# Merged loads and stores for queries, keys and mixed channels, and norm_g spread by TensorE in a one-core hybrid attention layer

## The chip, the cores and the metric

The kernel runs on one core of a Trainium2 chip. The metric is the time in microseconds (us) of one execution on the device. A core has five engines with a queue of instructions each, worked off in order: TensorE (PE in the profile; its weight loads are PEld), VectorE (DVE), ScalarE (ACT), GpSimd (POOL) and SyncE (SP). In this kernel SP issues all the DMA transfers.

## The reference, cut to what matters

One layer over 1024 tokens of 1024 channels, float32:

```python
h = rmsnorm(x, norm_g)
z = h @ w_in                                   # 1024 x 3886 columns, split in 14 parts
a = pool_mixer(pv) * silu(pg)                  # windows of 2, 4, 8, 16, mean minus the token itself
b = dsa_mixer(dq, dk, dv, iq, ik, iw) * silu(dg)   # 6 heads of 64, each query attends to its top 256 keys
c = fox_mixer(fq, fk, fv, log_sigmoid(ff + bf)) * silu(fg)   # 6 heads of 64, causal, forgetting bias
out = rmsnorm(x + concat([a, b, c]) @ w_out, final_g)
```

The top 256 keys of a query are found from an index score, a weighted sum over 8 heads of relu(iq . ik), among the keys of its own chunk of 64 tokens and those before it.

## The kernel before, in words

**Numbers.** Every float32 operand of a product is split into a high part (float32r, made by ScalarE) and a low part, the rest (made by VectorE or GpSimd). A product is then three passes of TensorE (`mm3`, L460): high by high, high by low, low by high.

**Planner.** `Plan` holds all instructions with a duration, a priority and the keys that they read and write. `schedule` is a list scheduler: at each step it takes, over all engines, the instruction that can start first by its prices, with the priority among those of one engine. The order that results is the order in which each engine's queue is filled. A DMA is priced by an issue time on SP (0.45 us in `ld`), a delay, its bytes by a rate (330 GB/s) and a landing time. Tiles have slots (a tag with a size, an offset and a number of slots); a tile that takes over a slot waits for the work on the one before.

**Stages.** First the tokens are normalised in 8 tiles of 128 (`norm`): the square sum on ScalarE (L509 for tile 0, L505 for the others), a multiplication with the factor and with `gb`, norm_g spread over 128 partitions (L515, VectorE, by halves), transposes (L522, TensorE), and the split into `hT` (L526, L527). `gb` is filled in two ways: its first half by a product of a row of ones with the row of norm_g (L415) and a copy (L417, ScalarE), its second half by a DMA that reads the same 2 KB for each of the 128 partitions (L418). Until the first tile is ready, 60 small products on constants (L408) run on TensorE at the lowest priority.

Then come the index scores (`idx_tile`), their top 256 (`search`: 32 rounds of counting, L772 on ScalarE and L777 on VectorE), and beside them the projections with the channels on the partitions (`chan`, 48 products of 512 columns for each 128 channels): keys and queries (`qkproj`), gates (`gate`) and the pool's values. `qkproj` makes the high part `nh` (L723) and the low part `nl` (L724) of 128 channels (a pair of heads) by 512 tokens and stores them to DRAM with two DMAs. `gate` applies tanh on ScalarE (L737) and a VectorE step (L739) in a tile `th`, of which there are two slots, and stores it. The pool mixer (`pool_tile`) loads the gate back into a tile `th`, multiplies (L1093) and stores the result to a DRAM tile `mx_p`.

Attention runs in 12 units: 2 kinds (f, d) x 3 pairs of heads x 2 halves g of the queries (512 tokens each). A unit needs the query tiles `qx` (high) and `ql` (low), both of shape 128 x 2 x 512, where index 1 is the head; each head's 64 channels are loaded into both halves of the partitions, so `load_q` issues 8 DMAs of 128 KB. The key tile `ks` holds for each head its high part in one half of the partitions and its low part in the other (`load_k`, 4 DMAs of 128 KB for 512 keys). The products L925 (with `qx`) and L928 (with `ql`) then give the logits; L936 (VectorE) adds the bias or mask and takes the maximum, L947 is the exponential, L962 the transposes, L969 and L971 the split of the weights, L975 and L980 the products with the values. At its end a unit multiplies with the gate and the softmax denominators, and stores 128 channels by 512 tokens to a DRAM tile `mx_f` or `mx_d`.

The output projection (`outproj`) takes 128 tokens at a time: 8 DMAs of 64 KB bring the 8 blocks of 128 channels from the 8 DRAM tiles, L1133 (ScalarE) and L1134 (GpSimd) split them, 48 products follow, L1146 adds x, and the final normalisation ends in a store.

Of the kernel before, what the change touches and what calls it, by code (L numbers as in the profile page):

```python
# [27 lines left out]
D = 1024  # L28
# [52 lines left out]
class Plan:  # L81
# [81 lines left out]
    def schedule(self):  # L163
# [10 lines left out]
        while len(order) < n:  # L174
# [49 lines left out]
            if e == SP:  # L224
                free[e] = t + o.dur
                st = max(t + 1.4, dma_free[0])
                dma_free[0] = st + o.bytes / 330e3
                o.end = dma_free[0] + 0.7
            else:
                free[e] = t + o.dur  # L230
                o.end = t + o.dur
# [60 lines left out]
def tile_trunk(ctx: ExitStack, tc: tile.TileContext, x, w_in, norm_g, pool_w, pool_scale,  # L292
# [15 lines left out]
    r1 = lay("R", 0, [("hT", 32 * KB, 2), ("Wh", 4 * KB, 2), ("Wl", 4 * KB, 2), ("nh", 2 * KB, 2), ("nl", 2 * KB, 2)])  # L308
# [4 lines left out]
    r3 = lay("R", r2, [("ks", 4 * KB, 3), ("qx", 4 * KB, 2), ("ql", 4 * KB, 2), ("ph", 2 * KB, 3), ("pl", 2 * KB, 2)], 2)  # L313
# [93 lines left out]
    for q in range(60):  # L407
# [3 lines left out]
    grow = P.new("gr", [1, 640])  # L411
    ld(lambda: grow()[:, :512], lambda: norm_g[0:1, 0:512], 2048, w=[(grow, 0)], pr=-101)
    G(lambda: nc.gpsimd.memset(grow()[:, 512:640], 1.0), 60, [], [(grow, 1)], -99)
    pb = P.new("pj", [128, 512])
    P.op(PE, lambda: nc.tensor.matmul(pb(), grow()[:, 512:640], grow()[:, 0:512], start=True, stop=True), 1.7,  # L415
         [(grow, 0), (grow, 1)], [pb], -99)
# [443 lines left out]
    mix_d = {}  # L860

    def load_k(kind, pair, u, pr):
        d = QKD[kind, pair, u]
        k = P.new("ks", [128, 2, 512], F32R)
        kk = [("qk", kind, pair, u, j) for j in range(2)]
        for e in range(2):
            ld(lambda e=e: k()[64 * e:64 * e + 64, 0, :], lambda e=e: d[e, 0:64, :], 131072, kk, [(k, 3 + e)], pr)
        ld(lambda: k()[0:64, 1, :], lambda: d[1, 64:128, :], 131072, kk, [(k, 1)], pr)
        ld(lambda: k()[64:128, 1, :], lambda: d[0, 64:128, :], 131072, kk, [(k, 2)], pr)
        return k  # L870

    def load_q(kind, pair, u, pr):
        d = QKD[kind, pair, u]
        kk = [("qk", kind, pair, u, j) for j in range(2)]
        qx = P.new("qx", [128, 2, 512], F32R)
        for s in range(2):
            for e in range(2):
                ld(lambda s=s, e=e: qx()[64 * e:64 * e + 64, s, :], lambda s=s: d[0, 64 * s:64 * s + 64, :], 131072,
                   kk, [(qx, s, e)], pr)
        ql = P.new("ql", [128, 2, 512], F32R)  # L880
        for s in range(2):
            for e in range(2):
                ld(lambda s=s, e=e: ql()[64 * e:64 * e + 64, s, :], lambda s=s: d[1, 64 * s:64 * s + 64, :], 131072,
                   kk, [(ql, s, e)], pr)
        return qx, ql
# [9 lines left out]
    def unit(kind, pair, g, ks, VV):  # L895
# [3 lines left out]
        qx, ql = load_q(kind + "q", pair, g, pr0)  # L899
        sm = P.new("sm", [128, 4, 2, 2])  # L900
        os = []
        for hd in range(2):
# [11 lines left out]
            for j in range(3, -1, -1):  # L914
                t = 4 * g + j
                Ps.insert(0, [])
                for u in range(g + 1):
# [6 lines left out]
                    kk = [(k, 3), (k, 4)] if hd == 0 else [(k, 1), (k, 2)]  # L924
                    M(lambda s=s, k=k, n=n, j=j, hd=hd: nc.tensor.matmul(  # L925
                        s()[:, :n], qx()[:, hd, j * 128:j * 128 + 128], k()[:, hd, :n], start=True, stop=False),
                      n, kk + [(qx, hd, 0), (qx, hd, 1)], [s], pr)
                    M(lambda s=s, k=k, n=n, j=j, hd=hd: nc.tensor.matmul(  # L928
                        s()[:, :n], ql()[:, hd, j * 128:j * 128 + 128], k()[:, hd, :n],
                        start=False, stop=True), n, kk + [(ql, hd, 0), (ql, hd, 1)], [s], pr)  # L930
# [118 lines left out]
    def pool_tile(m, consts):  # L1049
# [37 lines left out]
        for u in range(2):  # L1087
# [35 lines left out]
    def outproj(i, WO, fgb):  # L1123
# [3 lines left out]
        for k in range(KT):  # L1127
# [122 lines left out]
```

## Time and profile before

| | before |
|---|---|
| time, median of 3 runs (lowest to highest) | 661.5 us (658.8 to 661.52) |
| the profiled execution: its time, its span | 663.12 us, 661.4 us |
| mean granted TensorE clock | 0.992 |
| busy: PE, PEld, DVE, ACT, POOL | 626.0, 528.8, 473.6, 425.5, 197.8 us |
| DMA: packets, bytes, mean rate | 98438, 103.01 MB, 156 GB/s |

The span reaches from the first to the last instruction. Busy time is that of the engine's own instructions; the DMA share is the mean busy share of the core's 16 DMA engines. In the rows further down, `idle before <- releaser` says how long an engine stood before an instruction and what it waited for last; SPq is SP's queue, and its durations are those of issuing a DMA, not of its transfer. A DMA that lands counts as a releaser under the names of its two ends (`mx_p<-FA` is the store from the SBUF area FA to the DRAM tile mx_p). RA and FA are the two large SBUF areas in which the planner places tiles.

### The profile page before, as it was taken

The page shows a single profiled execution, that of the slowest core. Times are in us where ns is not written, and L with a number is a line of the kernel's source. Part 1 is how long each engine was busy: PE and PEld are TensorE (multiplying, and loading weights), DVE is VectorE, ACT ScalarE, POOL GpSimd, SP SyncE. Part 2 cuts the span into 40 slices and gives each one's busy share as a digit, 9 for nine tenths or more (in the row PEclk, how much of TensorE's full clock was granted, in tenths as well). Part 3 has the DMA queues.
Part 4 walks back from the last instruction along what each step waited for, and adds up shares of the span by engine and source line. Part 5 has one row for each costly group of instructions (what it writes and reads, how often), then busy time and mean ns, then how long its engine had stood idle before and what let it go on. Part 6 is the DMA issues. An engine that isn't in the chain of part 4 may idle for free. (4 is left out here: it accounts for less than half of the span.)

```text
span 661.4 us, 10577 instructions
## 1 busy us (share of the span) xinstructions
PE 626.0 (95%) x3278; PEld 528.8 (80%) x3278; DVE 473.6 (72%) x1187; ACT 425.5 (64%) x944; POOL 197.8 (30%) x218
## 2 busy tenths in 40 slices
PE   7899999999999999699999999999889899999995
PEld 5798777899888998487887887888768778888884
DVE  5888999877677887799995866757677667562322
ACT  5746688798888878422468576777658687842111
POOL 3510312630047340034253341520303370322311
PEclk9999999999999999899999999999999999999998
DMA  7826443560045346544468566759784762346311
GB/s 218 239 65 172 138 144 112 156 179 1 16 124 132 96 160 192 174 111 153 153 201 245 178 184 197 219 171 287 195 252 141 234 197 92 128 147 201 108 56 63
DMA packets 98438, 103.01 MB, mean 156 GB/s; under 512 B 10983, under 2 KB 67399, under 8 KB 98382
## 3 DMA queue, kind: packets, MB, share of 16 engines
q1 hardware_dynamic: 98382, 102.34, 51.8%
q8 instruction: 26, 0.43, 0.3%
q14 instruction: 30, 0.25, 0.1%
HBM read 72.35 MB, written 29.96 MB: 155 GB/s over the span
## 5 line engine op out<-in xcount | busy, mean ns | idle before, releaser
L462 PE MATMUL bank<-RA 128*128 128x512 f32 (+2 forms) x2016 | 484.5, 378 | 8.9 <-DVE FA L739 6.0
L462 PEld LDWEIGHTS bank<-RA 128*128 128x128 f32 x2016 | 360.7, 189 | 60.4 <-DVE FA L739 6.3
L772 ACT ACTIVATE FA<-FA 128x768 bf16<-128x768 f32 (+2 forms) x96 | 99.4, 1036 | 18.4 <-DVE FA L794 15.4
L695 POOL TENSOR_TENSOR RA<-FA,RA 128x512 fp32r<-128x512 f32 x44 | 63.1, 1446 | 137.0 <-ACT RA L694 127.9
L969 ACT ACTIVATE RA<-bank 128x512 fp32r<-128x512 f32 (+1 forms) x120 | 63.8, 553 | 53.5 <-PE bank L962 51.5
L936 DVE CUSTOM_DVE_ANT_0 FA<-bank,FA 128x512 f32<-128x512 f32 (+3 forms) x144 | 77.6, 551 | 28.1 <-PE bank L928 10.6
L947 ACT ACTIVATE FA<-FA 128x512 f32<-128x512 f32 (+3 forms) x144 | 86.7, 606 | 6.5 <-DVE FA L942 6.4
L971 DVE TENSOR_TENSOR RA<-bank,RA 128x512 fp32r<-128x512 f32 (+1 forms) x120 | 73.4, 632 | 23.6 <-ACT RA L969 22.8
L777 DVE TENSOR_SCALAR_CACHE_REDUCE FA<-FA 128x384 bf16<-128x384 f32 (+2 forms) x96 | 71.2, 742 | 1.9
L962 PE MATMUL bank<-FA 128*128 128x128 f32 x432 | 71.8, 273 | 0.1
L962 PEld LDWEIGHTS bank<-FA 128*128 128x128 f32 x432 | 54.4, 140 | 18.1 <-DVE RA L971 2.4
L925 PE MATMUL bank<-RA 128*128 128x512 f32 (+3 forms) x144 | 52.9, 368 | 3.5 <-DVE FA L936 3.5
L928 PE MATMUL bank<-RA 128*128 128x512 f32 (+3 forms) x144 | 51.0, 356 | 4.1 <-DMA RA<-qk_dq 4.0
L607 DVE SCALAR_TENSOR_TENSOR FA<-FA 128x512 f32<-128x512 f32 (+3 forms) x70 | 52.1, 762 | 2.4
L975 PE MATMUL bank<-RA 128*128 128x512 f32 (+3 forms) x144 | 45.8, 345 | 3.5 <-ACT RA L969 3.5
L599 ACT ACTIVATE FA<-bank 128x512 f32<-128x512 f32 (+3 forms) x80 | 40.1, 525 | 12.4 <-PE bank L595 6.1
L980 PE MATMUL bank<-RA 128*128 128x512 f32 (+3 forms) x144 | 48.0, 361 | 0.0
L932 POOL TENSOR_TENSOR FA<-FA 128x128 f32<-128x128 f32 x48 | 25.3, 535 | 64.4 <-DVE FA L936 46.0
L1013 POOL TENSOR_TENSOR FA<-FA 128x512 f32<-128x512 f32 x12 | 15.6, 1297 | 81.5 <-DVE FA L1009 58.9
L975 PEld LDWEIGHTS bank<-RA 128*128 128x128 f32 x144 | 26.7, 189 | 9.9 <-ACT RA L969 6.2
L925 PEld LDWEIGHTS bank<-RA 128*128 128x128 f32 x144 | 27.2, 189 | 9.0 <-DVE FA L936 5.1
L1146 DVE TENSOR_TENSOR FA<-bank,FA 128x512 f32<-128x512 f32 x16 | 11.0, 688 | 31.4 <-PE bank L462 31.4
(145 smaller groups left out, 678.5 us busy)
## 6 DMA issues: line engine op xcount, KB each, us to landing
FA<-in_w_in_dram SPq DMA_DIRECT2D x60, 256.0 KB, 3.8
FA<-in_x_dram SPq DMA_DIRECT2D x15, 512.0 KB
RA<-qk_fq SPq DMA_DIRECT2D x48, 128.0 KB, 3.7
RA<-qk_dq SPq DMA_DIRECT2D x48, 128.0 KB, 3.6
RA<-qk_dk SPq DMA_DIRECT2D x36, 128.0 KB, 3.3
FA<-in_w_out_dram SPq DMA_DIRECT2D x16, 256.0 KB, 3.2
out_dram<-FA SPq DMA_DIRECT2D x7, 512.0 KB, 2.6
RA<-qi SPq DMA_DIRECT2D x24, 128.0 KB, 3.1
```

What stands on the lines that cost most here:

```text
L462: M(lambda: nc.tensor.matmul(p()[:, :n], fa(), fb(), start=st, stop=sp), n, keys, [p], pr)
L607: V(lambda rl=rl, w=w, acc=acc, wc=wc: nc.vector.scalar_tensor_tensor(acc(), rl()[:, :w], wc(), acc(), op0=OP.mult, op1=OP.add), w, [rl, ( ...
L695: G(lambda raw=raw, s=s: nc.gpsimd.tensor_tensor(Wl()[:, s, :], raw(), f32(Wh()[:, s, :]), op=OP.subtract), 512, [raw, (Wh, kh)], [(Wl, kh ...
L772: A(lambda c=c, i=i, jk=jk, s=s: nc.scalar.activation(jk(), SC[i](), AF.Sign, bias=s(), scale=-1.0, accum_out=cn()[:, c:c + 1]), n, sck(i) ...
L777: V(lambda c=c, i=i, jk=jk, s=s: nc.vector.tensor_scalar(jk(), SC[i](), s(), None, op0=OP.is_lt, op1=OP.add, accum_out=cn()[:, c:c + 1]), ...
L925: M(lambda s=s, k=k, n=n, j=j, hd=hd: nc.tensor.matmul(s()[:, :n], qx()[:, hd, j * 128:j * 128 + 128], k()[:, hd, :n], start=True, stop=Fa ...
L936: V(lambda s=s, Pt=Pt, n=n, u=u, j=j, mx=mx, bias=bias: nc.vector.tensor_tensor_reduce(Pt()[:, :n], s()[:, :n], bias()[:, u * 512:u * 512 ...
L947: A(lambda Pt=Ps[j][u], n=n, j=j, u=u, hd=hd, nm=nm: nc.scalar.activation(Pt()[:, :n], Pt()[:, :n], AF.Exp, bias=nm()[:, j:j + 1], accum_o ...
L962: M(lambda pt=pt, j=j, d=d, Pt=Ps[j][kb // 4], c=kb % 4 * 128: nc.tensor.transpose(pt()[:, j * 128 - d:j * 128 - d + 128], Pt()[:, c:c + 1 ...
L969: A(lambda ph=ph, pt=pt, c=c: nc.scalar.activation(ph()[:, c], pt()[:, c], AF.Copy), n, [pt], [ph], pr, psum=True)
L971: V(lambda ph=ph, pl=pl, pt=pt, c=c: nc.vector.tensor_tensor(pl()[:, c], pt()[:, c], f32(ph()[:, c]), op=OP.subtract), n, [pt, ph], [pl], pr)
L975: M(lambda o=o, v=v, ph=ph, c=c, j0=j0, kb=kb: nc.tensor.matmul(o()[:, j0 * 128:], v(kb), ph()[:, c], start=(kb == 0), stop=False), 512 - ...
```

## The change

The stored high and low parts of queries and keys become one tile of two planes with one store; `load_q` and `load_k` read with access patterns that take the planes together (one DMA for each half of the partitions); the eight blocks of mixed channels lie in one DRAM tile for each half of the tokens, and `outproj` loads its 128 tokens of all of them with one DMA. The second half of `gb` is made like the first. In the planner the issue of a DMA is priced 0.6 instead of 0.45 us, its delay 1.6 instead of 1.4, the rate 270 instead of 330 GB/s, the landing 0.8 instead of 0.7.

```diff
@@ Plan.schedule @@
-                st = max(t + 1.4, dma_free[0])
-                dma_free[0] = st + o.bytes / 330e3
-                o.end = dma_free[0] + 0.7
+                st = max(t + 1.6, dma_free[0])
+                dma_free[0] = st + o.bytes / 270e3
+                o.end = dma_free[0] + 0.8
@@ slots @@
-    ... ("nh", 2 * KB, 2), ("nl", 2 * KB, 2)])
+    ... ("n", 4 * KB, 2)])
-    r3 = lay("R", r2, [("ks", 4 * KB, 3), ("qx", 4 * KB, 2), ("ql", 4 * KB, 2), ("ph", 2 * KB, 3), ("pl", 2 * KB, 2)], 2)
+    r3 = lay("R", r2, [("ks", 4 * KB, 3), ("q", 8 * KB, 2), ("ph", 2 * KB, 3), ("pl", 2 * KB, 2)], 2)
@@ ld @@
-        P.op(SP, fn, 0.45, r, w, pr, nbytes)
+        P.op(SP, fn, 0.6, r, w, pr, nbytes)
@@ norm_g @@
-    ld(lambda: grow()[:, :512], lambda: norm_g[0:1, 0:512], 2048, w=[(grow, 0)], pr=-101)
+    ld(lambda: grow()[:, :D], lambda: norm_g[0:1, :], 4096, w=[(grow, 0)], pr=-101)
...
-    A(lambda: nc.scalar.activation(gb()[:, 0:512], pb(), AF.Copy), 512, [pb], [(gb, 0)], -99, psum=True)
-    ld(lambda: gb()[:, 512:], lambda: bass.AP(tensor=norm_g.tensor, offset=norm_g.offset + 512,
-                                              ap=[[0, 128], [1, 512]]), 262144, w=[(gb, 1)], pr=-99)
+    for u in range(2):
+        pb = P.new("pj", [128, 512])
+        P.op(PE, lambda pb=pb, u=u: nc.tensor.matmul(pb(), grow()[:, D:], grow()[:, u * 512:u * 512 + 512], start=True,
+                                                     stop=True), 1.7, [(grow, 0), (grow, 1)], [pb], -99)
+        A(lambda pb=pb, u=u: nc.scalar.activation(gb()[:, u * 512:u * 512 + 512], pb(), AF.Copy), 512, [pb], [(gb, u)],
+          -99, psum=True)
@@ qkproj @@
-            ld(lambda: d[0], nh, 262144, r=[nh], w=[("qk", kind, pair, u, 0)], pr=PR_EV)
-            ld(lambda: d[1], nl, 262144, r=[nl], w=[("qk", kind, pair, u, 1)], pr=PR_EV)
+            ld(lambda: d.rearrange("l p c -> p l c"), hl, 524288, r=[(hl, 0), (hl, 1)], w=[("qk", kind, pair, u)],
+               pr=PR_EV)
@@ load_k @@
-        for e in range(2):
-            ld(lambda e=e: k()[64 * e:64 * e + 64, 0, :], lambda e=e: d[e, 0:64, :], 131072, kk, [(k, 3 + e)], pr)
-        ld(lambda: k()[0:64, 1, :], lambda: d[1, 64:128, :], 131072, kk, [(k, 1)], pr)
-        ld(lambda: k()[64:128, 1, :], lambda: d[0, 64:128, :], 131072, kk, [(k, 2)], pr)
+        for e in range(2):
+            ld(lambda e=e: k()[64 * e:64 * e + 64], lambda e=e: bass.AP(
+                tensor=d.tensor, offset=d.offset + e * 65536, ap=[[512, 64], [32768, 2], [1, 512]]), 262144,
+               [("qk", kind, pair, u)], [(k, e)], pr)
@@ load_q @@
-        (two tiles qx, ql; for each, for s in range(2), for e in range(2), a load of 131072 bytes)
+        q = P.new("q", [128, 4, 512], F32R)
+        for e in range(2):
+            ld(lambda e=e: q()[64 * e:64 * e + 64], lambda: bass.AP(
+                tensor=d.tensor, offset=d.offset, ap=[[512, 64], [32768, 4], [1, 512]]), 524288,
+               [("qk", kind, pair, u)], [(q, e)], pr)
@@ unit: both products now name both halves of k and of q @@
-                    kk = [(k, 3), (k, 4)] if hd == 0 else [(k, 1), (k, 2)]
+                    kk = [(k, e) for e in range(2)] + [(q, e) for e in range(2)]
@@ unit, pool_tile @@
-        ld(lambda: d, ot, 262144, ko, [("mix", kt, g)], pr)
+        ld(lambda: mix_d[g][kt], ot, 262144, ko, [("mix", kt, g)], pr)
@@ outproj @@
-        for k in range(KT):
-            ld(lambda k=k: m()[:, k, :], lambda k=k: mix_d[k, g][:, j * 128:j * 128 + 128], 65536, [("mix", k, g)],
-               [(m, k)], pr)
+        ld(m, lambda: bass.AP(tensor=mix_d[g].tensor, offset=mix_d[g].offset + j * 128,
+                              ap=[[512, 128], [65536, KT], [1, 128]]), 524288, [("mix", k, g) for k in range(KT)], [m], pr)
```

## Rows read from the trace of the kernel before

**Rows 1.** Stretches of 10 us: busy us (instructions) by engine, clock, DMA share, GB/s.
```profile
290.00:300.00 10.00, 10.00 (x46) 8.29 (x45) 9.89 (x19) 2.35 (x4) 3.37 (x3) 1.00 0.36 82
...
450.00:460.00 10.00, 10.00 (x65) 8.80 (x65) 8.33 (x25) 6.52 (x17) 1.29 (x1) 1.00 0.97 279
...
470.00:480.00 10.00, 8.16 (x55) 7.09 (x53) 5.00 (x16) 5.68 (x16) 3.81 (x3) 1.00 0.58 161
```

**Rows 2.** What PE waited for: us in total, times, longest.
```profile
PE bank L462 <- DVE FA L739: 6.0, 1, 6.0
PE bank L928 <- DMA RA<-qk_dq: 4.0, 2, 2.9
PE bank L925 <- DVE FA L936: 3.5, 3, 2.0
```

**Rows 3.** Timeline, 255 to 284 us: start, duration, engine, line, [idle before].
```profile
260.81 6.01 SPq L365 DMA_DIRECT2D RA<-qk_fq  x8
...
266.38 0.75 DVE L1093 SCALAR_TENSOR_TENSOR FA<-bank,FA 128x512 f32<-128x512 f32 x1
266.86 2.51 SPq L365 DMA_DIRECT2D RA<-qk_fk  x4
...
268.34 0.75 DVE L1093 SCALAR_TENSOR_TENSOR FA<-bank,FA 128x512 f32<-128x512 f32 x1
...
270.65 0.93 SPq L365 DMA_DIRECT2D mx_p<-FA  x2
271.11 0.19 ACT L772 ACTIVATION_READ_ACCUMULATOR FA<-FA 128x1 f32 x1
...
274.90 1.30 ACT L737 ACTIVATE FA<-bank 128x512 f32<-128x512 f32 x2 [3.61 <-DMA mx_p<-FA]
...
276.27 7.91 PE L462 MATMUL bank<-RA 128*128 128x512 f32 x22 [6.01 <-DVE FA L739]
```

**Rows 4.** Stretches of 2 us, PE alone: length, busy (products), clock, DMA share, GB/s.
```profile
276.27:278.00 1.73, 1.73 (x4) 0.50 0.39 152
278.00:280.00 2.00, 2.00 (x6) 0.50 0.34 131
280.00:282.00 2.00, 2.00 (x7) 0.53 0.02 7
```

**Rows 5.** The start: DMA rates of 0 to 13 us in 40 slices, then timeline.
```profile
GB/s 0 0 0 0 0 6 57 227 397 347 378 252 221 145 82 76 50 214 246 302 296 288 339 348 358 341 302 217 157 123 89 105 142 302 281 136 142 189 215 257
...
2.30 2.07 PE L415 MATMUL bank<-FA 1*128 1x512 f32 x2
...
5.28 0.58 ACT L417 ACTIVATE FA<-bank 128x512 f32<-128x512 f32 x1
...
8.24 0.75 DVE L515 SCALAR_TENSOR_TENSOR FA<-FA 128x512 f32<-128x512 f32 x1 [0.55 <-DMA FA<-in_norm_g_dram]
...
9.76 1.06 ACT L505 ACTIVATE FA<-FA 128x1024 bf16<-128x1024 f32 x1 [3.90 <-DMA FA<-in_x_dram]
...
12.82 0.41 PE L462 MATMUL bank<-RA 128*128 128x302 f32 x1 [2.26 <-ACT RA L526]
```

**Rows 6.** The loads of queries, one kind: SP's ns min/median/max, first and last start.
```profile
L365 SPq DMA_DIRECT2D RA<-qk_dq x48: 444/594/1921, 401.6 to 516.3; - x48
```

**Rows 7.** Loads of 512 KB: one kind's median landing; one issue in the timeline.
```profile
FA<-nf_d SPq DMA_DIRECT2D x6, 512.0 KB, 4.1
...
543.64 0.38 SPq L365 DMA_DIRECT2D FA<-in_x_dram  x1
```

**Rows 8.** Timeline, 596 to 616 us: the first tile of the second half.
```profile
601.61 1.27 SPq L365 DMA_DIRECT2D FA<-mx_d  x3
...
603.66 1.06 ACT L1133 ACTIVATE RA<-FA 128x1024 fp32r<-128x1024 f32 x1 [2.27 <-issue]
...
604.80 2.40 POOL L1134 TENSOR_TENSOR RA<-FA,RA 128x1024 fp32r<-128x1024 f32 x1 [2.60 <-ACT RA L1133]
...
610.39 0.69 DVE L1146 TENSOR_TENSOR FA<-bank,FA 128x512 f32<-128x512 f32 x1 [4.75 <-PE bank L462]
```

More of the change, by code (lines that the diff above doesn't have):

```diff
@@ L306, in lay @@
         return base
-    r1 = lay("R", 0, [("hT", 32 * KB, 2), ("Wh", 4 * KB, 2), ("Wl", 4 * KB, 2), ("nh", 2 * KB, 2), ("nl", 2 * KB, 2)])
+    r1 = lay("R", 0, [("hT", 32 * KB, 2), ("Wh", 4 * KB, 2), ("Wl", 4 * KB, 2), ("n", 4 * KB, 2)])
     lay("R", 0, [("WO", 32 * KB, 2)], 3)
@@ L410, in tile_trunk @@
     gb = P.new("gb", [128, D])
[L411 to L419 removed]
+    grow = P.new("gr", [1, D + 128])
+    ld(lambda: grow()[:, :D], lambda: norm_g[0:1, :], 4096, w=[(grow, 0)], pr=-101)
+    G(lambda: nc.gpsimd.memset(grow()[:, D:], 1.0), 60, [], [(grow, 1)], -99)
+    for u in range(2):
[4 more added lines that the diff above has]
+          -99, psum=True)
     ld(bfb, lambda: bass.AP(tensor=fox_bf.tensor, offset=fox_bf.offset, ap=[[0, 128], [1, NH]]), 3000, w=[k_bfb],
@@ L857, in small_masks @@
               PR_SEL)
-    mix_d = {}
+    mix_d = [dram(f"mix{g}", [KT, 128, 512]) for g in range(2)]
     def load_k(kind, pair, u, pr):
@@ L873, in load_q @@
         d = QKD[kind, pair, u]
-        kk = [("qk", kind, pair, u, j) for j in range(2)]
-        qx = P.new("qx", [128, 2, 512], F32R)
-        for s in range(2):
-            for e in range(2):
[L878 to L885, printed above, removed]
+        q = P.new("q", [128, 4, 512], F32R)
[3 more added lines that the diff above has]
+               [("qk", kind, pair, u)], [(q, e)], pr)
+        return q
     unit_no = [0]
@@ L898, in unit @@
         pr0 = PR_AT + unit_no[0] * 0.01
-        qx, ql = load_q(kind + "q", pair, g, pr0)
+        q = load_q(kind + "q", pair, g, pr0)
         sm = P.new("sm", [128, 4, 2, 2])
@@ L923, in unit @@
                     k = ks[u]
-                    kk = [(k, 3), (k, 4)] if hd == 0 else [(k, 1), (k, 2)]
+                    kk = [(k, e) for e in range(2)] + [(q, e) for e in range(2)]
                     M(lambda s=s, k=k, n=n, j=j, hd=hd: nc.tensor.matmul(
-                        s()[:, :n], qx()[:, hd, j * 128:j * 128 + 128], k()[:, hd, :n], start=True, stop=False),
-                      n, kk + [(qx, hd, 0), (qx, hd, 1)], [s], pr)
+                        s()[:, :n], q()[:, hd, j * 128:j * 128 + 128], k()[:, hd, :n], start=True, stop=False),
+                      n, kk, [s], pr)
                     M(lambda s=s, k=k, n=n, j=j, hd=hd: nc.tensor.matmul(
-                        s()[:, :n], ql()[:, hd, j * 128:j * 128 + 128], k()[:, hd, :n],
-                        start=False, stop=True), n, kk + [(ql, hd, 0), (ql, hd, 1)], [s], pr)
+                        s()[:, :n], q()[:, 2 + hd, j * 128:j * 128 + 128], k()[:, hd, :n],
+                        start=False, stop=True), n, kk, [s], pr)
                     if dg:
@@ L1094, in pool_tile @@
                                                                   op1=OP.mult), 512, [py, gt, kps], [gt], pr)
-            d = dram(f"mx_p{m}{u}", [128, 512])
-            ld(lambda d=d: d, gt, 262144, [gt], [("mix", m, u)], pr)
-            mix_d[m, u] = d
+            ld(lambda u=u, gt=gt: mix_d[u][m], gt, 262144, [gt], [("mix", m, u)], pr)
     def load_wo():
@@ L1126, in outproj @@
         m = P.new("m", [128, KT, 128])
-        for k in range(KT):
-            ld(lambda k=k: m()[:, k, :], lambda k=k: mix_d[k, g][:, j * 128:j * 128 + 128], 65536, [("mix", k, g)],
-               [(m, k)], pr)
+        ld(m, lambda: bass.AP(tensor=mix_d[g].tensor, offset=mix_d[g].offset + j * 128,
+                              ap=[[512, 128], [65536, KT], [1, 128]]), 524288, [("mix", k, g) for k in range(KT)], [m], pr)
         mh = P.new("mh", [128, KT, 128], F32R)
         ml = P.new("ml", [128, KT, 128], F32R)
-        km = [(m, k) for k in range(KT)]
+        km = [m]
         A(lambda: nc.scalar.activation(mh(), m(), AF.Copy), 1024, km, [mh], pr)
```

12 lines of the change are left out of this document (4 added, 8 removed).

## The prediction

> **What bounds the kernel now.** The first view is the busy time by stretches of 10 us. TensorE (PE) is busy 10.00 of 10 us in most of them, at a granted clock of 1.00 [rows 1]. Over the span of 661.4 us, by the page's first part, it is busy 626 us. So the kernel is bound by PE, and a DMA edit can win only from the 35.4 us in which PE stands idle, or from time in which it runs at a lower clock. The end takes its share whatever is done, since a normalisation, a store and the closing waits follow the last product. So does the start: until 12.82 us PE has only transposes and the 60 warm-up products (L408) to do [rows 5].
>
> The second view is the list of what PE waited for. The longest wait is one of 6.0 us for line L739, the gate's VectorE step; then come 4.0 us for loads of queries (`qk_dq`, two waits) and 3.5 us for the bias step L936 [rows 2]. The third view is the timeline around the 6.0 us, because this wait ends in a DMA: PE stands for L739, L739 for the tanh L737, and L737 stood 3.61 us for the store `mx_p`, whose source tile it overwrites [rows 3]. The second of the two pool tiles behind these stores was finished at 269.09 (L1093), yet both stores went out at 270.65 and after, because SP, one queue in order, was still issuing eight loads of `qk_fq` (6.01 us), four of `qk_fk` (2.51 us), and after them two of weights [rows 3]. This is the place that the change touches most. It costs more than its 6.0 us. From 276.27 to 282 the granted clock is about half, 0.50 to 0.53, which of the two levels is 1.2 GHz; 4 + 6 + 7 = 17 products begin in these 5.73 us [rows 4], where 46 in 10 us make 3.70 us for 17 at full clock [rows 1]: another 2.0 us. The event costs 8.0 us in all.
>
> **The change part by part.**
>
> *norm_g.* One load of 4 KB takes the place of one of 2 KB, the 256 KB broadcast load goes, and a second pair of products L415 (2.07 us) and a second copy L417 (0.58 us) come [rows 5]. PE fills that time with warm-up products today, so the products cost nothing; without that cover they would cost 2.07 us. ScalarE does nothing between the end of L417 at 5.86 and L505 at 9.76, so the copy is hidden too. The second products end at about 4.37 + 2.07 = 6.4, the copy at 7.0, before the first L515 ends at 8.24 - 0.55 = 7.69, so the second L515 starts at about 7.7 and not 8.24. That alone moves nothing, because what is late next is the x tile: L505 waited 3.90 us for it, ScalarE then splits weights, and L526 releases PE at 12.82 after an idle 2.26 us [rows 5]. The tile lay behind the broadcast load in the same queues. 262,144 bytes at some 250 GB/s, the mean of slices 8 to 28 in the row of rates, are 1.05 us; four of these slices (14 to 17, 0.325 us each) move only 50 to 145 GB/s, and if they are the broadcast, its removal gives more [rows 5]. Below is 0, if ScalarE's order puts other work first; above is the gap of 2.26. I take **-1.0**, the bytes by the rate.
>
> *Query, key loads and their stores.* Per unit of attention eight query loads become two, and per key tile four become two; each pair of stores becomes one. No byte is saved: 1 MB per unit and the same runs of 2 KB. What is saved is SP's time: one 128 KB load held SP a median of 594 ns, 444 at least [rows 6]. How long one of 512 KB in this form holds it no row shows. Between the 444 ns of the shortest and four times the median (2.4 us, if it goes by bytes) I take the median, 0.6 us, because a 512 KB load of x took 0.38 us, so bytes don't set it [rows 7]. The twelve loads at 260.81 to 269.37 then become four of 0.6, 2.4 us in place of 8.5. Their 1.57 MB need 5.6 us at 279 GB/s, the rate of the busiest stretch [rows 1], so the data ends near 266.5 and no longer stands before a store that leaves at 269.1. From the second store's issue (about 271.2) to L737 there were 3.7 us [rows 3]: from 269.1 this gives 272.8, 2.1 us sooner. If L737 needs only the first store (its tile was done at 267.13), ScalarE's own work is late next: L772 ends at 271.30, so L737 gains 3.6 us. With a gap of 2.4 to 3.9 us the clock may hold: between 470 and 480 PE stood idle 1.84 us net, one wait of it 2.9 us long crossing into the next stretch, at 1.00 [rows 1, 2]; then 2.0 us come back. The term lies between -2.1 and -5.6; I take **-4.5**, with the clock and the middle of the two waits. It falls to 0 if the stores are held by something else than SP's issues.
>
> At the start of each unit the first product L925 waited, of the eight query loads, for two; L928 for six; now both wait for all. In the dense stretch at 279 GB/s [rows 1], 1 MB takes 3.76 us, 256 KB 0.94 and 768 KB 2.8: the data for L925 comes up to 2.8 us later, for L928 0.9 us. Against it stand the issues: the sixth of eight loads leaves SP after 6 x 0.59 = 3.5 us, the second of two after 1.2. The two nearly cancel at L928, and L925 is hidden where the other head's work lies before it; no wait of L925 for a load is in the list [rows 2]. I take **0**, between -4.0 (the whole present wait) and +11.2 (the last rival).
>
> A load of 512 KB has one completion for all its rows. The Trainium skill (DMA: Bandwidth & Descriptors, "Why a DMA increments its semaphore by 16 and not by 1") says that only the full count means that all data has landed, and that an intermediate value does not tell which bytes have. By that rule the loads cannot be used piecewise, and it speaks against merging them; by the waits in the trace, 4.0 us in two places, the pieces are of little use as they are, and the sum has 0. If the rule decided in each unit, the result would be the last rival's.
>
> *Stores and the merged channels.* The qk store now waits for the low part too, one VectorE step (L724), and holds a tile of two; the next projection of the same kind needs 24 products, 24 x 0.217 = 5.2 us [rows 1], so this costs 0. Eight 64 KB loads per output tile become one of 512 KB that waits for the last of eight stores. This bites once, at tile 4, the first of the second half: the last three loads are issued at 601.61, its low part L1134 ends at 604.80 + 2.40 = 607.2, and PE starts on it when L1146 is released at 610.39 [rows 8], a slack of 3.2 us. All 512 KB after 601.6 land, by the 4.1 us of a 512 KB load of `nf_d` [rows 7], at 605.7; with 1.06 us of L1133 and 2.40 of L1134, 609.2. The slack is still 1.2 us: **0**, up to +1.5 if the 512-byte pieces are slower.
>
> *The planner's prices* (issue 0.45 to 0.6, 330 to 270 GB/s, landing later) change no instruction but the order of all queues. I put **0**: no row prices it, and both outer rivals below are what it can do.
>
> **Sum.** -1.0 - 4.5 = -5.5 us. On the profiled execution (663.1 us, span 661.4 and 1.7 around it) that is 657.6. It was 1.6 us over the median of 661.5, so on the median 656.0.
>
> **Rivals.**
>
> 1. *The wait for the store stays.* The issues get shorter, but the stores sit behind the queries' data in the queues, or another tile's reuse takes their place: the DMA share is already 0.97 in a stretch such as 450 to 460 [rows 1]. For it: no byte is saved. Against it: SP issued loads without pause just then. Only norm_g is left: 661.5 - 1.0 = 660.5. It is also the case in which one merged load holds SP as long as those that it replaces.
> 2. *The dearer prices cure more.* The planner then puts fewer instructions ahead of data that is still under way; the waits of 4.0 us for queries and 3.5 us at L936 [rows 2] go too: 656.0 - 7.5 = 648.5. For it: L505 and L737 both stood at the head of ScalarE's queue for a DMA [rows 3, 5], as in a plan that expects data too early. Against: with dearer loads work that hides waits can be put elsewhere.
> 3. *Slower: units wait for whole queries.* The place is the first L925 of a unit between 440 and 530, where DMA is dense; the price the 2.8 us of data by which L925 then waits longer. Two such units (5.6) eat the gain, from there it is slower; four make 11.2 - 5.5 = +5.7: 667.2. For it: L928 waits there already [rows 2]. Against: both query tiles are loaded a unit ahead.
>
> **How the numbers follow.** The forecast, 656.0, has 0.44 and a range of its own of 652 to 660 (terms between -2 and -9 less the join). Rival 1 (660.5) has 0.20, rival 2 (648.5) 0.18, rival 3 (667.2) 0.18. A measurement of this kernel can tell about 0.5%, 3.3 us, from no change: faster is under 658.2, slower over 664.8. Faster: 0.38 of the forecast's 0.44, all of rival 2, 0.02 of rival 1: 0.58. Slower: 0.16 of rival 3 and 0.02 of late mishaps at the join: 0.18. The rest, 0.24, is no change. The range 647 to 667 leaves out the lower part of rival 2 and the upper half of rival 3, some 0.18.
>
> **What would show it.** Right: the first L462 near 11.8; in the stretch where the pool's stores meet the gates, SP done with the queries before the stores are ready, L737 not idle for a store by over 2 us, no stretch at half clock. The step on queries is wrong if PE's list shows L925 waiting for `qk_` loads for more than 4.0 us; the join if the first tile of the second half stands for L1134. The whole is wrong if PE's idle time grows in other places by as much as it falls here.

## The result and the profile after

After the change the median is 658.1 us (656.8 to 661.3, 10 runs) against 661.5 (658.6 to 666.8, 10 runs): a ratio of 0.9936, with an interval of 0.9908 to 0.9964. The profiled execution took 658.86 us with a span of 657.1 (663.12 and 661.4 before). PE's busy time did not fall (629.4 us after, 626.0 before), and its mean clock is 0.986 after, 0.992 before.

Following VectorE's steps through both traces gives where the 4.3 us of span come from. The last L545 of the index stage begins at 52.6 instead of 53.5 (-0.9). The event near 270 gives back 1.1, but a new wait of 0.7 us for `qk_fq` stands at 260. The rest, some -3.0 by this sum, comes in the attention between 300 and 600, where the prediction had nothing.

The line numbers of the code behind the change lie 1 to 11 lower: L737 is now L736, L739 L738, L772 L771, L925 L919, L936 L930, L947 L941, L962 L956, L969 L963, L1093 L1085, L1133 L1122, L1134 L1123, L1146 L1135. First, what PE waits for after (us in total, times, longest), beside [rows 2]:

```profile
PE bank L462 <- DVE FA L738: 4.7, 1, 4.7
...
PE bank L956 <- ACT FA L941: 1.3, 2, 0.7
PE bank L969 <- ACT RA L963: 1.3, 1, 1.3
PE bank L919 <- DVE FA L930: 1.1, 1, 1.1
...
PE bank L919 <- DMA RA<-qk_fq: 0.7, 1, 0.7
```

The wait for the gate is still the longest, 4.7 instead of 6.0. The 4.0 us for `qk_dq` are gone, and the bias step holds PE for 1.1 instead of 3.5. The timeline of after around the longest wait answers to [rows 3]:

```profile
261.35 1.24 SPq L365 DMA_DIRECT2D RA<-qk_fq  x2
263.75 1.97 SPq L365 DMA_DIRECT2D FA<-in_w_in_dram  x2
...
266.52 2.59 SPq L365 DMA_DIRECT2D mix<-FA  x2
268.00 0.75 DVE L1085 SCALAR_TENSOR_TENSOR FA<-bank,FA 128x512 f32<-128x512 f32 x1
...
271.47 1.15 ACT L771 ACTIVATE FA<-FA 128x1024 bf16<-128x1024 f32 x1
272.52 0.19 ACT L771 ACTIVATION_READ_ACCUMULATOR FA<-FA 128x1 f32 x1
...
273.18 1.29 ACT L736 ACTIVATE FA<-bank 128x512 f32<-128x512 f32 x2 [0.47 <-DMA mix<-FA]
274.56 11.73 PE L462 MATMUL bank<-RA 128*128 128x512 f32 x38 [4.67 <-DVE FA L738]
```

SP is free in time: its two query loads take 1.24 us, and the two stores go out at 266.52 and 268.77, right after the steps that make their tiles (the second L1085 ends at 268.75), instead of at 270.65 and 271.20. But the tanh L736 starts only at 273.18. ScalarE works on counting steps L771 up to 272.71 and stands idle for the last 0.47 us. What ends last is the store: L736 waits for the first of the two, and by the trace's semaphore counts that one lands at 273.16, 6.6 us after its issue. In the kernel before it landed at 274.88, 4.2 us after its issue at 270.65. So it was issued 4.1 us sooner and landed 1.7 us sooner. The two query loads issued ahead of it landed at 268.80 and 271.44. Without the counting steps L736 would have started no sooner; a store that landed earlier could have gained 0.47 us more, up to their end. And the clock falls after the gap, as before. After, by 2 us (columns of [rows 1]):

```profile
274.00:276.00 2.00, 1.45 (x3) 1.16 (x4) 2.00 (x7) 0.48 (x1) 0.00 (x0) 0.50 0.33 128
276.00:278.00 2.00, 2.00 (x6) 1.61 (x5) 2.00 (x7) 0.60 (x1) 0.00 (x0) 0.50 0.37 138
278.00:280.00 2.00, 2.00 (x6) 1.52 (x6) 2.00 (x3) 0.29 (x1) 0.00 (x0) 0.50 0.00 0
280.00:282.00 2.00, 2.00 (x9) 1.63 (x8) 2.00 (x3) 0.34 (x1) 1.43 (x1) 0.86 0.34 131
```

From 274.56 to 282, 3 + 6 + 6 + 9 = 24 products begin in 7.44 us; at 0.217 each they need 5.2, so 2.2 us are lost to the clock. The event costs 4.7 + 2.2 = 6.9 us, where it cost 8.0.

The start of after, beside [rows 5]: the row of rates over the first 13 us (0.325 us a slice), then the timeline.

```profile
GB/s 0 0 0 0 0 13 19 183 384 391 378 208 101 164 239 164 208 246 353 350 377 290 309 269 199 222 156 252 340 326 337 297 166 141 96 191 268 381 416 416
```

```profile
7.53 1.06 ACT L505 ACTIVATE FA<-FA 128x1024 bf16<-128x1024 f32 x1 [0.60 <-DMA FA<-in_x_dram]
...
12.04 1.90 PE L462 MATMUL bank<-RA 128*128 128x302 f32 x12
```

L505 starts at 7.53 instead of 9.76 and the first L462 at 12.04 instead of 12.82. At the other end, the first tile of the second half [rows 8]:

```profile
592.87 2.83 SPq L365 DMA_DIRECT2D FA<-mix  x3
...
599.22 3.00 POOL L1123 TENSOR_TENSOR RA<-FA,RA 128x1024 fp32r<-128x1024 f32 x1 [1.21 <-ACT RA L1122]
...
606.19 0.69 DVE L1135 TENSOR_TENSOR FA<-bank,FA 128x512 f32<-128x512 f32 x1 [4.75 <-PE bank L462]
```

L1123 ends at 602.2, 4.0 us before L1135 at 606.19: no wait at the join.

Last, two long stretches (columns of [rows 1]), before and then after:

```profile
300.00:500.00 200.00, 189.83 (x1056) 157.93 (x1055) 146.68 (x394) 130.01 (x341) 60.43 (x75) 1.00 0.69 203
500.00:540.00 40.00, 38.12 (x211) 31.03 (x209) 28.12 (x69) 31.28 (x74) 18.88 (x14) 1.00 0.63 195
```

```profile
300.00:500.00 200.00, 196.72 (x1095) 165.52 (x1096) 150.53 (x399) 135.03 (x353) 70.79 (x81) 1.00 0.77 208
500.00:540.00 40.00, 36.58 (x191) 29.10 (x189) 30.67 (x81) 32.64 (x81) 13.56 (x10) 0.91 0.80 221
```

Between 300 and 500 PE begins 39 more matrix instructions than before and idles 6.9 us less. Between 500 and 540 it begins 20 fewer, at a clock of 0.91. So one place of the attention gains and another gives back.

### The profile page after: what moved, and what is told of

Same layout as the page of the kernel before. It is cut to its first block, busy times and chain, and to the rows that moved or that the text cites. A ratio compares the mean times of both kernels' runs of the same rounds, so it can differ in the third digit from the quotient of the medians.

```text
span 657.1 us, 10265 instructions
## 1 busy us (share of the span) xinstructions
PE 629.4 (96%) x3280; PEld 532.3 (81%) x3280; DVE 478.8 (73%) x1187; ACT 426.9 (65%) x945; POOL 198.6 (30%) x218
## 5 line engine op out<-in xcount | busy, mean ns | idle before, releaser
L462 PE MATMUL bank<-RA 128*128 128x512 f32 (+2 forms) x2016 | 480.9, 378 | 4.7 <-DVE FA L738 4.7
L462 PEld LDWEIGHTS bank<-RA 128*128 128x128 f32 x2016 | 361.0, 189 | 55.4 <-DVE FA L738 5.1
L771 ACT ACTIVATE FA<-FA 128x768 bf16<-128x768 f32 (+2 forms) x96 | 99.5, 1037 | 20.1 <-DVE FA L793 15.9
L963 ACT ACTIVATE RA<-bank 128x512 fp32r<-128x512 f32 (+1 forms) x120 | 64.1, 552 | 58.5 <-PE bank L956 57.9
L695 POOL TENSOR_TENSOR RA<-FA,RA 128x512 fp32r<-128x512 f32 x44 | 59.5, 1364 | 128.3 <-ACT RA L694 127.7
L930 DVE CUSTOM_DVE_ANT_0 FA<-bank,FA 128x512 f32<-128x512 f32 (+3 forms) x144 | 77.3, 552 | 23.2 <-PE bank L922 14.3
L941 ACT ACTIVATE FA<-FA 128x512 f32<-128x512 f32 (+3 forms) x144 | 86.7, 606 | 8.5 <-DVE FA L936 8.3
L956 PE MATMUL bank<-FA 128*128 128x128 f32 x432 | 72.8, 278 | 3.7 <-DVE RA L965 2.2
L956 PEld LDWEIGHTS bank<-FA 128*128 128x128 f32 x432 | 54.7, 143 | 21.0 <-DVE RA L965 5.6
L919 PE MATMUL bank<-RA 128*128 128x512 f32 (+3 forms) x144 | 52.3, 364 | 2.7 <-DVE FA L930 1.1
L969 PE MATMUL bank<-RA 128*128 128x512 f32 (+3 forms) x144 | 46.4, 349 | 2.7 <-DVE FA L1003 1.4
L926 POOL TENSOR_TENSOR FA<-FA 128x128 f32<-128x128 f32 x48 | 28.6, 600 | 58.2 <-DVE FA L930 47.5
L1135 DVE TENSOR_TENSOR FA<-bank,FA 128x512 f32<-128x512 f32 x16 | 11.0, 689 | 34.6 <-PE bank L462 33.9
L969 PEld LDWEIGHTS bank<-RA 128*128 128x128 f32 x144 | 27.4, 191 | 8.5 <-ACT RA L963 3.0
L919 PEld LDWEIGHTS bank<-RA 128*128 128x128 f32 x144 | 27.4, 191 | 8.2 <-DVE FA L930 2.2
```

The lines of the kernel that those rows point to most:

```text
L462: M(lambda: nc.tensor.matmul(p()[:, :n], fa(), fb(), start=st, stop=sp), n, keys, [p], pr)
L695: G(lambda raw=raw, s=s: nc.gpsimd.tensor_tensor(Wl()[:, s, :], raw(), f32(Wh()[:, s, :]), op=OP.subtract), 512, [raw, (Wh, kh)], [(Wl, kh ...
L771: A(lambda c=c, i=i, jk=jk, s=s: nc.scalar.activation(jk(), SC[i](), AF.Sign, bias=s(), scale=-1.0, accum_out=cn()[:, c:c + 1]), n, sck(i) ...
L919: M(lambda s=s, k=k, n=n, j=j, hd=hd: nc.tensor.matmul(s()[:, :n], q()[:, hd, j * 128:j * 128 + 128], k()[:, hd, :n], start=True, stop=False),
L930: V(lambda s=s, Pt=Pt, n=n, u=u, j=j, mx=mx, bias=bias: nc.vector.tensor_tensor_reduce(Pt()[:, :n], s()[:, :n], bias()[:, u * 512:u * 512 ...
L941: A(lambda Pt=Ps[j][u], n=n, j=j, u=u, hd=hd, nm=nm: nc.scalar.activation(Pt()[:, :n], Pt()[:, :n], AF.Exp, bias=nm()[:, j:j + 1], accum_o ...
```

## Experiments

Each was timed in five rounds against the kernel before. The ratio is that to the kernel before in the same rounds. Median in us (lowest to highest, runs), ratio with its interval:

| run | time | ratio |
|---|---|---|
| e1_prices_only | 656.1 (655.4 to 657.8, 10) | 0.9920 (0.9896 to 0.9944) |
| e2_old_prices | 663.2 (660.3 to 664.9, 12) | 1.0014 (0.9988 to 1.0040) |
| e3_pieces | 660.4 (658.9 to 661.9, 12) | 0.9969 (0.9942 to 0.9996) |
| e4_broadcast_back | 660.1 (658.3 to 663.8, 12) | 0.9986 (0.9961 to 1.0011) |
| e5_halves_in_turn | 657.4 (655.7 to 658.1, 6) | 0.9933 (0.9910 to 0.9956) |
| e6_own_slots | 651.6 (651.0 to 654.0, 5) | 0.9856 (0.9830 to 0.9881) |
| e7_prices_norm_g | 654.2 (652.8 to 655.3, 6) | 0.9890 (0.9865 to 0.9915) |
| e9_both | 648.9 (648.1 to 649.2, 4) | 0.9807 (0.9781 to 0.9833) |
| e10_priced_as_pieces | 657.8 (654.4 to 660.3, 12) | 0.9935 (0.9906 to 0.9965) |
| e11_mixed_merged | 647.0 (645.7 to 647.3, 6) | 0.9784 (0.9744 to 0.9823) |
| e12_stores_merged | 655.7 (654.6 to 656.5, 12) | 0.9925 (0.9900 to 0.9950) |
| e13_loads_merged | 654.9 (654.5 to 656.7, 9) | 0.9916 (0.9888 to 0.9944) |

The comparisons between two of these rows below are of medians. From the ratios and their intervals (taken as independent) follows how sure they are: prices 5.2 us, own slots 6.5 and 5.3, and the 8 to 9 us of e12 and e13 are clear; e4 against after is 3.3 us and e7 against after 3.0, each give or take 2.5. Those of e3 against after (2.2), e7 against e1 (2.0) and e11 against e9 (1.5) are smaller than their own uncertainty of 2.3 to 3.1 us.

**The planner's prices.** e1 gives the kernel before the new prices and nothing else; e2 gives the kernel after the old ones.

```diff
-                st = max(t + 1.4, dma_free[0])
-                dma_free[0] = st + o.bytes / 330e3
-                o.end = dma_free[0] + 0.7
+                st = max(t + 1.6, dma_free[0])
+                dma_free[0] = st + o.bytes / 270e3
+                o.end = dma_free[0] + 0.8
...
-        P.op(SP, fn, 0.45, r, w, pr, nbytes)
+        P.op(SP, fn, 0.6, r, w, pr, nbytes)
```

> The kernel before with only the planner's new DMA prices (0.6, 1.6, 270, 0.8). Theory: the 2 to 3 us that the attention stage gained came from the new order, not from the merged loads: then this alone is at 658.5 to 659.5 (before 661.5), with less idle PE between 300 and 600 us than the 12.4 us of before. Rival: the merged loads did it, so this stays within 1.5 us of 661.5, or is slower.

> The changed kernel (658.1) with the old prices of the planner. Theory (the order of the new prices gave the attention gain): it loses 2 to 3 us, 660 to 661; the start keeps its 0.9 us. Rival (merged loads gave it): it stays at 657.5 to 658.5.

The prices alone take 5.2 us from the kernel before (661.3 in these runs), more than its theory had. Without them the rest of the change is at 663.2, slower than either expectation of e2 and not to be told from no change against before; giving after its prices is worth 5.1. So the prices measure the same with and without the rest. What PE waits for in e1 (lines as in the kernel before):

```profile
PE bank L462 <- DVE FA L739: 3.8, 1, 3.8
...
PE bank L925 <- DVE FA L936: 1.3, 2, 0.8
```

and in e2:

```profile
PE bank L969 <- DMA RA<-vd: 5.0, 1, 5.0
...
PE bank L919 <- DMA RA<-qk_fq: 3.7, 1, 3.7
...
PE bank L462 <- DVE FA L738: 1.4, 1, 1.4
```

In e1 no row of the list names a `qk_` load any more (4.0 us before), the bias step holds PE for 1.3 instead of 3.5, and the gate for 3.8 instead of 6.0, with all loads in pieces. In e2, with merged loads, the gate holds PE for only 1.4, but PE stands for data again: 5.0 us for `vd`, and 3.7 at the start of a unit for its whole query load. This agrees with rival 2's mechanism, that with dearer transfers the planner puts less work ahead of data that is under way. That the mechanism, and not any other difference between the orders, makes the 5 us is not shown: the four prices were changed together, and the orders differ in more than these waits.

**Merging and norm_g with the order held.** e3 and e4 keep the order of the kernel after on every engine. e3 sends each query and key load as pieces of 128 KB; e4 loads norm_g's second half by broadcast as well, into a place that nothing reads. Their lines lie 6 and 5 higher than those of after (in e3 L468 is L462, L744 is L738, and L371 issues the pieces; in e4 L510 is L505, L467 is L462).

```diff
-        for e in range(2):
-            ld(lambda e=e: q()[64 * e:64 * e + 64], ..., 524288, [("qk", kind, pair, u)], [(q, e)], pr)
+        for h in range(2):
+            lds([(lambda e=e, s=s: q()[64 * e:64 * e + 64, s, :], ...)
+                 for s in (2 * h, 2 * h + 1) for e in range(2)], 524288, [("qk", kind, pair, u)], [(q, h)], pr)
```

> The changed kernel with its order on every engine untouched, but each merged load of queries (512 KB) sent as four of 128 KB and each of keys (256 KB) as two of 128 KB, the two halves of the partitions in turn, as in the kernel before: 156 issues on SP in place of 42. Theory A (SP's issue time was what the merging saved): +2 to +3 us, 660 to 661, and waits of L919 or L922 for query loads appear. Theory B (the data is the bound, and a load into one half of the partitions moves slower than two in turn): no loss or up to 1.5 us faster, 656.5 to 658.1; the stretches of 250 to 270 and 430 to 480 us move 270 to 290 GB/s in place of 230 to 275, and the landing of queries falls under 6 us from 7.5 to 8.

```diff
+        def fx(u=u):
+            nc.sync.dma_start(xt0()[:, u * 512:u * 512 + 512], x[0:128, u * 512:u * 512 + 512])
+            if u:
+                nc.sync.dma_start(FA[:, spare:spare + 512], bass.AP(
+                    tensor=norm_g.tensor, offset=norm_g.offset + 512, ap=[[0, 128], [1, 512]]))
```

> The changed kernel with its order untouched, plus the 256 KB broadcast load of norm_g at its old place on SP (behind the halves of the first x tile), its data unused. Theory: the load's time on the queues delays the second x tile and the weights by 1.0 us, so the first L462 comes 0.8 to 1.2 us later (12.04 to about 13) and the last L545 of the index stage 0.9 us later (52.8 to 53.7): 659.0. Rival: the stage is bound by VectorE, the delay is absorbed by 50 us, and the time is 658.1.

The pieces cost 2.3 us (660.4 against 658.1; by the ratios 0.0033, 2.2 us). Timeline of e3:

```profile
264.61 5.08 SPq L371 DMA_DIRECT2D RA<-qk_fq  x8
...
270.96 0.93 SPq L365 DMA_DIRECT2D mix<-FA  x2
...
276.34 9.95 PE L468 MATMUL bank<-RA 128*128 128x512 f32 x35 [6.69 <-DVE FA L744]
```

Eight pieces hold SP until 269.7, the stores leave at 270.96, and the gap is 6.69 instead of 4.67, 2.0 us more. Other waits of PE differ in this execution too: 2.4 us more at one line, and the 0.7 and 0.9 us for `qk_fq` and `vd` gone. So theory A had the time right, but not its other sign, as no product waits for a query load. Theory B's signs fail but for the landing, 2.7 to 2.8 us a piece: the dense stretches move less than in after (212 against 236 GB/s in 250 to 270, 232 against 247 in 430 to 480). So the step on SP's queue is seen in the trace, at its lower bound of 2.1; the medians agree with it but are no proof of their own.

The broadcast costs 2.0 us by the medians, more than its theory's 0.9. Start of e4:

```profile
GB/s 0 0 0 0 0 13 63 113 372 403 372 233 139 120 69 76 101 95 158 258 328 353 332 318 337 362 354 323 243 133 80 65 138 145 274 253 170 164 224 289
```

```profile
10.09 1.06 ACT L510 ACTIVATE FA<-FA 128x1024 bf16<-128x1024 f32 x1 [3.17 <-DMA FA<-in_x_dram]
...
13.15 0.41 PE L467 MATMUL bank<-RA 128*128 128x302 f32 x1 [1.20 <-DVE FA L486]
```

The slow slices are back: 120, 69, 76, 101, 95, where after has 164, 239, 164, 208, 246. The x tile is 2.6 us later, the first product 1.1, and the last step of the index stage 3.2 in this execution.

**How the halves of a query load are sent.** e5 replaces the two 512 KB loads, each of which fills one half of the partitions, by four of 256 KB with the halves in turn, the order again held.

> The changed kernel (658.1), its order on every engine untouched; the two query loads of 512 KB, each into one half of the partitions, are sent as four of 256 KB into the two halves in turn. Theory (one half of the partitions at a time limits the rate): the landing of queries falls from 8 to 9 us to under 6, the dense stretches reach 270 to 290 GB/s, and the time is 656.5 to 658. Rival (the rate is the queues' own, and SP's issues count): landing stays at 7 us or more for the last piece, SP issues 24 loads more, and the time is 658 to 659.

It is 657.4, which the noise doesn't tell from 658.1, so the time decides nothing between the two. Loads after (engine, count, KB, median us from issue to landing), then of e5:

```profile
RA<-qk_fq SPq DMA_DIRECT2D x12, 512.0 KB, 9.0
RA<-qk_dq SPq DMA_DIRECT2D x12, 512.0 KB, 8.1
```

```profile
RA<-qk_fq SPq DMA_DIRECT2D x24, 256.0 KB, 4.9
RA<-qk_dq SPq DMA_DIRECT2D x24, 256.0 KB, 6.6
```

The medians are of each piece, and the last piece of a tile counts. The dense stretches move 244 and 258 GB/s (236 and 247 in after), short of the 270 to 290 of the theory, and the gap near 270 is still 4.5 us. The wait of 0.7 us for `qk_fq` is gone. So filling half of the partitions at a time is at most a small cost.

**What holds the event.** e6 takes away the reason for the wait: the pool's gate tile gets a slot of its own, so that L736 (L737 in e6) overwrites nothing that a store still reads. e7 adds to e1 the norm_g part alone, all transfers of queries, keys and mixed channels in pieces; e9 is e7 with the own slots.

```diff
+    P.tag("pg", "F", 2 * KB, [f1, f1 + 2048], 1)
...
-            gt = P.new("th", [128, 512])
+            gt = P.new("pg", [128, 512])
```

> The changed kernel, but the four gate tiles of the pool get two slots of their own in place of those of the tanh L736, so the tanh no longer waits for a store of mixed channels. The planner orders anew. Theory (that wait, as the planner saw it, put the tanh behind the counting rounds; it is the root of the 4.67 us gap and of the half clock after it): PE has no gap over 1.5 us and no clock under 0.9 between 262 and 290; -5 to -7 us, 651 to 653. Rival (ScalarE's and VectorE's counting rounds hold PE there whatever the slots): a gap of 3 us or more stays within that stretch and the time is 656 to 658.

> The kernel before with the new prices (656.1 alone) and norm_g spread by TensorE, loads and stores of queries, keys and mixed channels in pieces as before. If norm_g is worth what the added broadcast cost (2.0 us) in every order: 654.1, and the merging of loads is then worth 4 us on the wrong side (658.1 against 654.1). Rival (its worth depends on the order): 656 to 658, and merging costs nothing.

> As the kernel with new prices and norm_g but pieces, with own slots for the pool's gate tiles. If the own slots are worth 5 to 7 us in any order and the pieces are no worse than the merged loads: 648 to 650, faster than both kernels. Rival: the stall moves to the next wait of that stretch (loads of queries hold SP until 270, so the stores and the key loads behind them are late): 653 to 656.

Timeline of e6, and PE alone by 10 us (busy, instructions, clock, DMA share, GB/s):

```profile
262.07 0.58 ACT L737 ACTIVATE FA<-bank 128x512 f32<-128x512 f32 x1
...
269.56 0.60 ACT L737 ACTIVATE FA<-bank 128x512 f32<-128x512 f32 x1
```

```profile
260.00:270.00 10.00, 9.68 (x40) 1.00 1.07 260
270.00:280.00 10.00, 10.00 (x46) 1.00 0.40 133
```

The tanh now stands between counting steps, PE is full, and the clock stays at 1.00, although the DMA share between 260 and 270 is 1.07 (1.08 in after). The event's 6.9 us are gone and the time falls by 6.5 (658.1 to 651.6). The edit takes away the wait and remakes the order at once, so the two are not separated; in pieces it gains 5.3 (e7 to e9), so it holds in two orders. e7 shows that after's other parts cost time: without the merging it is 654.2, so that, going from e7 to after, merging queries, keys and mixed channels adds 3.9. With own slots the same comparison is 648.9 to 651.6, +2.7.

**Which merging.** e10 is after with the merged loads priced on SP like the pieces that they replace (0.6 us each); theory: the planner, told that a merged load is cheap, issues too much too early. e11 to e13 start from e9 and merge one thing at a time.

```diff
-        P.op(SP, fn, 0.6, r, w, pr, nbytes)
+        P.op(SP, fn, 0.6 * n, r, w, pr, nbytes)
```

> The changed kernel, its merged loads of queries and keys sent merged, but priced by the planner as the pieces were: 2.4 us of SP for a query load, 1.2 for a key load. The difference of 3.9 us between pieces (654.2) and merged (658.1) under the same prices needs a cause. Theory (cheap merged loads let the planner start them in a burst ahead of what the tanh and the pool wait for; the order is the cause): 654 to 656, the gap near 270 under 3.5 us. Rival (the transfers of 512 KB themselves land late and fill the queues, whatever the order): 657 to 659.

> The fastest so far (648.9: new prices, norm_g by TensorE, own slots for the pool's gate tiles, query and key loads in pieces) plus the eight blocks of mixed channels in one tensor with one load per output tile. If this part of the merging is free, as forecast for the join at the first tile of the second half: 648 to 650. Rival (output tiles now wait for the last of eight stores, so less output work is there to fill attention's gaps): 650 to 652.

> The fastest so far (646.95: new prices, norm_g by TensorE, own slots for the pool's gate tiles, mixed channels merged, queries and keys in pieces) plus one store for high and low parts of queries and keys. With queries and keys wholly merged the same kernel took 651.6. Theory: the loads cost the 4.7 us, the stores nothing: 646 to 648. Rival: the store, which now waits for the low part and holds both planes until 512 KB are away, costs: 649 to 652.

> The other half: loads of queries and keys merged (two each), stores in pieces, the rest as in the fastest so far. Theory (the merged loads cost, by landing 8 us and more after their issue): 650.5 to 652.5. Rival (the stores): 646 to 648.5.

In e10 the gap near 270 falls to 2.8 us, as its theory had it: there the first store lands 4.0 us after its issue (266.25 to 270.24). But the time stays at 657.8, so the theory does not account for the 3.9. With own slots:

| q, k stores | q, k loads | mixed channels | time |
|---|---|---|---|
| pieces | pieces | pieces | 648.9 (e9) |
| pieces | pieces | merged | 647.0 (e11) |
| merged | pieces | merged | 655.7 (e12) |
| pieces | merged | merged | 654.9 (e13) |
| merged | merged | merged | 651.6 (e6) |

Merged mixed channels gain 1.9 us by the medians, within the noise. Merged stores cost 8.8, merged loads 8.0, both together 4.7; e12 and e13 are both slower than their theory and their rival had it. Prices of operations would add up; these do not. And in e12 no row of PE's list names a transfer; its largest waits in the attention are for the steps of a unit's own chain:

```profile
PE bank L962 <- ACT FA L947: 3.3, 5, 0.9
PE bank L975 <- ACT RA L969: 3.0, 3, 1.5
```

So PE is not held by late data there; what is left is the order that the planner made. e11 is the best version, 14.5 us under the kernel before. Where the difference arises, in e11 and then e12 (columns of [rows 1]):

```profile
300.00:500.00 200.00, 199.05 (x1121) 167.15 (x1120) 154.16 (x417) 141.87 (x372) 71.43 (x81) 1.00 0.71 215
500.00:540.00 40.00, 37.69 (x206) 30.05 (x204) 31.77 (x81) 32.12 (x78) 12.60 (x8) 0.96 0.61 173
```

```profile
300.00:500.00 200.00, 198.73 (x1112) 166.75 (x1111) 151.40 (x406) 136.52 (x356) 72.74 (x81) 1.00 0.69 212
500.00:540.00 40.00, 33.51 (x164) 25.81 (x163) 28.13 (x72) 32.56 (x81) 11.52 (x8) 0.87 0.58 173
```

Up to 500 they are alike; from 500 to 540 e12 begins 42 fewer instructions. After has the same thing, more mildly. Its PE timeline, then PE by 2 us:

```profile
523.72 0.44 PE L956 MATMUL bank<-FA 128*128 128x128 f32 x2 [0.67 <-ACT FA L941]
...
525.03 0.44 PE L956 MATMUL bank<-FA 128*128 128x128 f32 x2 [0.63 <-ACT FA L941]
526.73 0.79 PE L969 MATMUL bank<-RA 128*128 128x512 f32 x1 [1.27 <-ACT RA L963]
```

```profile
526.00:528.00 2.00, 1.21 (x3) 0.58 0.70 236
528.00:530.00 2.00, 2.00 (x10) 0.50 0.83 252
530.00:532.00 2.00, 2.00 (x6) 0.50 0.77 223
```

At the end of a d unit PE has nothing left but that unit's chain: exponential, transposes, split, product, with ScalarE in it. Three waits of 0.6 to 1.3 us follow each other, and then the clock is 0.50 for some 4 us. e12 has two such falls and e11 one. The kernel before has none there: it has projections (L462) between the unit's products, and one wait, after which the clock is still 1.00:

```profile
521.29 0.50 PE L975 MATMUL bank<-RA 128*128 128x512 f32 x1 [1.88 <-ACT RA L969]
```

The Trainium skill (TensorE: Matmul & The Clock Gate, "A second HAM failure mode: psum-queue depth-cycling") says, of a kernel that cycles through PSUM banks, that frequent small pauses between groups of products made the clock swing between its two levels. The rows of after agree, with pauses of another origin: the longest of these waits is 1.27 us, and the clock goes from 1.00 to 0.50.

## Why the prediction was right or wrong, point by point

The total, 656.0, came within 2.1 us, and faster was right; but that is luck. The parts by the runs: prices -5.2 (e1), norm_g -1.9 (e1 to e7), merging +3.9 (e7 to after), -3.2 in all by the medians. They were forecast at 0, -1.0 and -4.5: errors of -5.2, -0.9 and +8.4 nearly cancel. The other way round, norm_g and merging come first, together +1.9 (e2), and the prices then give -5.1.

- **norm_g, forecast -1.0: right in kind, too small.** Measured -1.9 (e7, not clear of the noise by itself) and -2.0 (e4). The step that failed is "the bytes by the rate": the broadcast does not move at 250 GB/s. The prediction had seen slices 14 to 17 at 50 to 145 GB/s and left them as "gives more"; e4 shows that they were the broadcast.
- **Query and key loads at the event, forecast -4.5: mis-sized.** The event gave 1.1 and left a wait of 0.7. (By its own words, "the clock and the middle of the two waits", the term is 2.0 and the middle of 2.1 and 3.6, so -4.9; the slip changes nothing here.) SP's part was right: 0.62 us a load against 0.6, stores out as soon as their tiles were done, 2.0 us of gap by e3. Of its two cases, that L737 needs only the first store was the true one. The step that failed is "the data ends near 266.5 and no longer stands before a store": the query loads landed at 268.80 and 271.44, in queues with a share of 1.08 between 260 and 270, and the store landed 6.6 us after its issue and not 3.7. Rival 1 named this ("the stores sit behind the queries' data"). "ScalarE's own work is late next" was off as well, 272.71 against 271.30, but did not end last. The gap shrank by 1.3, and with 4.7 us of it the clock fell again, so the 2.0 us for it did not come back. e6 shows that the whole event was to be had, by another edit.
- **Start of a unit, forecast 0: right in this order.** L919 waits once for `qk_fq`, 0.7 us; the 4.0 us for `qk_dq` went, but they go with the prices alone too (e1). Rival 3's +2.8 a unit did not occur, although 512 KB land 8 to 9 us after their issue: the tiles are loaded a unit ahead. With the old prices it did, once: in e2 a unit waits 3.7 us for `qk_fq`.
- **Stores and the join, forecast 0: right.** The slack is 4.0 us, 1.2 were forecast. As an edit by itself the merged mixed load gains 1.9 by the medians (e9 to e11), within the noise; where in the trace it gains was not followed further.
- **Planner's prices, forecast 0: the error that counts.** They are the largest single part. "No row prices it" was no reason for 0: the waits of 4.0 and 3.5 us for work issued ahead of its data stood in [rows 2], and they are what rival 2 was made of. That they go or shrink (e1) is shown; that the 5.2 us come from them is argued.
- **What the merging does to the order, forecast 0.** With the order held, sending the query and key loads merged is worth -2.3 (e3, by the medians); with the order remade, all merging together is worth +3.9. Why merged transfers lead this planner to worse orders stays open: it is not the issue price of the query and key loads (e10), and stores and loads each do it alone (e12, e13); e5 held the order and says nothing of it. A merged tile also has coarser dependencies, as a product then names both halves of keys and queries and a slot is held until the one store has landed; whether these lead the planner there was not tested. That any change of the planner's input scatters the time by such amounts fits all runs, but was not tested by itself.

## What to carry to other kernels

Where a planner orders the work, a constant in its prices is an edit like any other, and here was the larger one: time it alone, and hold the order when an edit's own worth is asked. Before a store is hurried, look at what is under way ahead of it: this one left SP 4.1 us sooner and landed 1.7 us sooner. A slot of its own for one tile removed the wait that faster issues only shortened. And an edit that the order turns to a loss can be left out of the mix: the best version here keeps the new prices, norm_g by TensorE and the merged mixed channels, adds the own slots, and leaves queries and keys in pieces (647.0 us).

## What the runs showed of the hardware

- Issuing a load held SP for as long whether it had 128 KB (median 0.59 us, [rows 6]) or 512 KB (0.60 and 0.59 us for the two kinds of query loads after).
- Landing does not go by size alone: 512 KB landed 4.1 us after the issue for `nf_d` ([rows 7]) and 8 to 9 us for the merged query loads. In pieces of 128 KB and the same order each landed after 2.7 to 2.8 us (e3), but eight of them took 5.08 us to issue.
- The same 256 KB store landed 6.6 us after its issue behind 1 MB of merged query loads (after), and after 4.0 to 4.2 us in the kernel before, e3 and e10.
- A 256 KB broadcast of one 2 KB row pulled all transfers to 69 to 120 GB/s for about 1.6 us and cost the kernel 2.0 us by the medians (e4).
- The granted clock fell to half not only after one long gap (4.7 us) but also after waits of 0.67, 0.63 and 1.27 us within 4 us. After a single wait of 1.88 us in the kernel before it stayed at 1.00.
